# The end of the gates in a hybrid attention block: the last two units' first products, the first heads' operands, the shifts' scores and the gate blocks are placed anew

## Chip, cores, metric

One core of a Trainium2 chip runs the whole block as one program. The metric is the device time of one execution in microseconds; lower is better. Before: 1523.75 us, the median of 3 runs (1515.12 to 1528.22).

## What is computed

One layer of a streaming encoder, 1024 frames of 1024 channels, all in float32. The reference, cut to its skeleton:

```python
h = rms_norm(x, norm1)
qa, ka, va, fa, qc, kc, vc, gates = split(h @ w_in)
o_a = forgetting_attention(qa, ka, va, log_sigmoid(fa + b))   # 8 heads, causal per frame
o_b = chunk_band_attention(qc, kc, vc, rel_bias)              # 8 heads, own and 8 earlier chunks of 64
g_a, g_b = split(sigmoid(gates))
x = x + (g_a * (o_a @ w_branch_a) + g_b * (o_b @ w_branch_b)) @ w_out
x = x + square(relu(rms_norm(x, norm2) @ w_up)) @ w_down
return rms_norm(x, final_norm)
```

What matters here is the boundary between the projection of the gates (2048 channels, 16 blocks of 128) and the attention of the 16 heads.

## The kernel before, in words

**Precision.** Every matrix product is made of two rounded parts of each operand, high and low: hi*hi, hi*lo and lo*hi, so each product of 128 x 128 by 512 is three matmuls (`product`, L211 to L219, the matmul in L218). `split` (L276) makes the parts of an activation, `split_w` (L162) those of a weight: the high part by a copy on ScalarE (L165), the low part by a subtraction (L167), on GpSimd here.

**Units.** The projections run in units of a Strassen-like scheme with seven products (`strassen_steps`, L521). A unit makes two blocks of 128 channels, each in two halves of 512 frames. Its products use the activation operands B11, T2, T1, T3, B21, B22, T4 in this order (`PRODS`) and four PSUM banks; a product is 4 chunks times 3 matmuls, 12 in all. Behind product 0 ScalarE copies the bank (p1), behind products 1 to 3 VectorE adds (L554, L556, L558), behind product 3 a block of output is done, behind product 4 another, behind 5 and 6 an addition (cc, L566) and a block each. `strassen_w` (L172) makes the seven weights from four loaded quarters, with additions on GpSimd (L188, L190, L205, L208) and splits; with `cut` it makes the first two, and the others later from a second load.

**Gates.** Eight units make the gates; `gate_out` (L388) multiplies a block by the frames' norm, takes the sigmoid on ScalarE (L391) and stores it to DRAM. The multiplication (L390) is on VectorE, but for three of the last unit's four blocks (`GPOOL`), which are on GpSimd. Units 0 to 5 come first. Then unit 7's first two products, then unit 6's, then the rest of 7 (L635 to L647). T2 and B11 have their own stack (`xtop`), which is closed when five of unit 6's products have been traced (`EARLY` 6); into that place go the qk tiles of the first two heads (`apq`, 8 KB a partition each, `load_head` L480, 1 MB through GpSimd's queue).

**Shifts.** Ahead of a head's attention the kernel computes a bound of each query's scores (`shifts`, L485): for each of 8 query blocks one or two score pieces of 128 x (128 to 512) on TensorE (L498), each reduced to its least value with the bias by VectorE out of PSUM (L505); then the 8 columns are transposed (L510), split and stored as a row to DRAM (`m_rows`, L513). For a head of the band kind the pieces are 256, 256, 384, 512 and four times 384 + 256 columns, 12 in all. While the attention of head n runs, the shifts of head n + 2 are made; those of the first two heads (`ahead`) are called two steps at a time between the remaining products of units 6 and 7 (`AHEAD` 2), and their banks come from the second half of PSUM (`psd[1]`).

**Attention.** `load_rest` (L693) loads sk (the low parts and the mask rows), v3 (the values) and, last, the shift row from `m_rows` (L700), all through GpSimd's queue. `attend` (L705) makes scores (L725, L733, L741), exponentials (L745), splits them (L277, L278) and accumulates the values (L748 to L750). `forget_columns` (L443) makes eight small transpositions (L449) of the forget sums, which heads 8 to 15 use; it stands ahead of the first head. sk and v3 of both first heads lie in pools that are opened after the operands of the projections have been released (L658). `branch` and `filler` (L667, L682) are products of the band branch that are spread over later heads; their weights (ab) are split when a filler is traced.

**Who sets the order.** A planner orders each engine's instructions by its own estimate of when they are ready; the order in which the program traces them decides between those that are. An instruction given through `TO` (TensorE), `VO` or `AO` is kept behind everything traced before it on its engine; the others may be moved. On the chip each engine takes its instructions in that fixed order. Tiles in released memory wait for the last user of what lay there (`reuse_waits="tile"`).

Of the kernel before, what the change touches and what calls it, by code (L numbers as in the profile page):

```python
# [11 lines left out]
F32 = mybir.dt.float32  # L12
# [6 lines left out]
P = 128  # L19
# [15 lines left out]
EARLY, AHEAD = 6, 2  # L35
# [8 lines left out]
GPOOL = (7,)  # L44
# [38 lines left out]
def hybrid_block(ctx: ExitStack, tc: tile.TileContext, xT, xN, g1, wall, wf, fb, relb, relt, rows, g2, g3, outT):  # L83
# [304 lines left out]
    def gate_out(ps, c, h, eng=V):  # L388
        t = etile("zt")
        eng.tensor_tensor(t, ps, rstd[:, hs(h)], op=ALU.mult)  # L390
        A.activation(t, t, AF.Sigmoid)  # L391
        store(z_dram[c, :, hs(h)], t)
# [92 lines left out]
    def shifts(pr, hh, qk, bc, ps_s, ps_t):  # L485
# [3 lines left out]
        for i in range(8):  # L489
# [17 lines left out]
            if i < 7:  # L507
                yield
        pt = ps_t.tile([P, HALF], F32, tag="d", name="mt")
# [11 lines left out]
    def strassen_steps(u, ps_pool, mk, out, start=(), between=None, before=None, cut=0):  # L521
# [9 lines left out]
        for b in (0, 2, 3, 1) if between else range(4):  # L531
            banks[b] = ps_pool.tile([P, HALF], F32, tag="d", name=f"u{u}_{b}")
# [5 lines left out]
        for i, (n, ks) in enumerate(steps):  # L538
            if i >= cut:
                yield  # L540
            if cut and i == cut:
# [3 lines left out]
            product(banks[b], first and 0 in ks, [((wh[:, k, :], wl[:, k, :]), xop[xn, k]) for k in ks],  # L545
                    3 not in ks)
# [21 lines left out]
        if before:  # L568
            before[1]()
            for a in late:  # L570
                out_(*a)

# [39 lines left out]
    def project_gate(g, **kw):  # L612
        return strassen_steps(U_GATE + g, psd[1 - next(units) % 2], etile,
                              lambda row, h, src: gate_out(src, 2 * g + row, h,
                                                          G if g in GPOOL and (row, h) != (0, 0) else V), **kw)

# [18 lines left out]
    last = project_gate(7, cut=2)  # L635
    next(last)
    steps = project_gate(6)
# [20 lines left out]
    ap_, apv, apq2, ap0 = [pool(astack, n, "right") for n in ("ap", "apv", "apq2", "ap0")]  # L658
# [8 lines left out]
    def branch(ps_pool, b, c, h):  # L667

        if h == 0:
            ab_w[b, c] = [split_w(quarter(U_AB + c // 2, ((0, 1), (3, 2))[c % 2][b]), f"ab{c}_{b}")]  # L670
# [15 lines left out]

    v3 = [apv.tile([P, 8, 3, HD], F32R, tag=f"v3{hh}", name=f"v3{hh}") for hh in range(2)]
    for hh in range(2):
        V.memset(v3[hh][:, :, 2, :].bitcast(F32), 1.0)

    sks = [ap_.tile([SK, 2, S], F32R, tag=f"sk{n}", name=f"sk{n}") for n in range(2)]

    def load_rest(pr, hh):  # L693
        sk = sks[hh]
        if pr % 4 == 0:
            load_r(sk[HD:SK - 2], rows[pr // 4, 0:16])
            load_r(sk[SK - 2:SK, 0, :], rows[pr // 4, 16:18, 0, :])
        load_r(sk[0:HD], sk_dram[2 * pr + hh])
        load_r(v3[hh][:, :, 0:2, :].rearrange("p c a d -> p c (a d)"), v_dram[pr, hh])
        load_r(sk[SK - 2:SK, 1, :], m_rows[2 * pr + hh])  # L700
        return sk
# [3 lines left out]
    def attend(pr, hh, sk, qk, nb):  # L705
# [4 lines left out]
        for h in range(2):  # L710
# [5 lines left out]
            for n, (j, b0, b1) in enumerate(chunks):  # L716
# [8 lines left out]
                T.matmul(ps[:, c], qk[:, 0, keys], qk[:, 1, qs], start=True, stop=False)  # L725
# [37 lines left out]
                yield  # L763
# [21 lines left out]
    forget_columns()  # L785
    rest, steps = load_rest(*heads[0]), iter(())
    for n, hd in enumerate(heads):
        sk, more = rest, iter(())
        if n < 15:
            rest = load_rest(*heads[n + 1])  # L790
        if n < 14:
            tiles.append((load_head(*heads[n + 2]), *load_bias(*heads[n + 2])))
            more = shifts(*heads[n + 2], *tiles[-1][:2], pss, psg)
# [371 lines left out]
```

## Time and profile before

| | us |
|---|---|
| median of the runs | 1523.75 |
| the profiled execution, its own time | 1524.15 |
| its span | 1522.4 |
| TensorE busy (matmuls) | 1462.8 |
| VectorE, ScalarE, GpSimd busy | 950.0, 733.9, 869.1 |
| mean granted clock of TensorE | 0.979 |
| first score piece of the shifts starts | 408.05 |
| last gate product's last matmul starts | 427.71 |
| first attention score (L725) starts | 439.34 |
| first exponential (L745) starts | 441.56 |

The rows are from one profiled execution. PE is TensorE, PEld its weight loads, DVE VectorE, ACT ScalarE, POOL GpSimd, SP the sync engine; a name with q behind it is that engine's queue of issues. A row of the timeline gives start, duration, engine, line, operation, tiles (written <- read), shapes and count; a bracket tells how long the engine had been idle and what released it. Matmul rows overlap by their pipeline, so a rate is read from the distance of two starts.

### The profile page before, as it was taken

What the parts mean: (1) busy time and instruction counts of PE and PEld (TensorE: products, weight loads), DVE (VectorE), ACT (ScalarE), POOL (GpSimd) and SP (SyncE); (2) the same over time, 40 slices, a digit from 0 to 9 for tenths busy, and PEclk for the clock granted to TensorE, in tenths of its full rate; (3) what the DMA queues carried; (4) which work ended last, traced back from release to release, by engine and by line L of the source; (5) the groups of instructions that cost most, each with busy time, mean ns of one, the idle gap of its engine ahead of it and who ended that gap; (6) DMA issues with size and microseconds to landing.
All of it is one profiled execution on the core that took longest, in us unless ns stands there. A gap on an engine that the chain in (4) does not pass through costs nothing.

```text
span 1522.4 us, 20991 instructions
## 1 busy us (share of the span) xinstructions
PE 1462.8 (96%) x6774; PEld 1212.7 (80%) x6774; DVE 950.0 (62%) x1528; ACT 733.9 (48%) x1392; POOL 869.1 (57%) x708
## 2 busy tenths in 40 slices
PE   7999999999888999999999999999999899999996
PEld 5777888888778887888787888888888688888885
DVE  7756555643366777765425677666666457999543
ACT  8533333343358777667425444333333344444653
POOL 2478877777742322121096468888887445567462
PEclk9999999999989899999999999999999999999998
DMA  8546668763589678876567324444443856588363
GB/s 271 151 116 184 190 194 231 195 187 119 173 192 187 156 158 188 200 202 154 165 196 226 127 79 170 152 153 151 153 152 135 278 189 202 155 253 222 97 208 110
DMA packets 153039, 267.18 MB, mean 175 GB/s; under 512 B 22552, under 2 KB 40216, under 8 KB 149792
## 3 DMA queue, kind: packets, MB, share of 16 engines
q1 hardware_dynamic: 78544, 141.02, 30.7%
q10 hardware_dynamic: 50448, 84.27, 17.5%
q0 software_dynamic: 23936, 40.54, 12.5%
q8 instruction: 53, 0.87, 0.2%
q14 instruction: 58, 0.48, 0.1%
HBM read 179.42 MB, written 86.34 MB: 175 GB/s over the span
## 4 chain that ended last, share of the span: by engine, by line
PE 73%; DMA 10%; DVE 6%; POOL 5%; issue 4%; ACT 2%; SPq 0%; ACTq 0%; DVEq 0%; POOLq 0%
PE u L218 36%; PE dS L218 11%; PE dA L218 8%; PE o L218 4%; DMA qk<-qk_dram 3%; PE m L218 2%; DMA wr<-wall 2%; DMA rb<-r_dram 2%; PE pv L748 2%; PE s L498 2%; PE pv L749 1%; PE pv L750 1%; PE st L725 1%; PE st L733 1%; PE dA L96 1%
## 5 line engine op out<-in xcount | busy, mean ns | idle before, releaser
L167 POOL TENSOR_TENSOR wl_A<-wr,wh_A 128x512 fp32r<-128x512 f32 x118 | 166.4, 1418 | 82.1 <-ACT wh_A L165 66.5
L167 POOL TENSOR_TENSOR wl_S<-S,wh_S 128x512 fp32r<-128x512 f32 x102 | 141.1, 1388 | 30.6 <-ACT wh_S L165 30.5
L278 DVE TENSOR_TENSOR tl<-p,th 128x512 fp32r<-128x512 f32 (+1 forms) x192 | 108.8, 586 | 31.2 <-ACT th L277 28.7
L165 ACT CAST wh_A<-wr 128x512 fp32r<-128x512 f32 x105 | 65.0, 620 | 102.0 <-DMA a_dram<-at 52.3
L165 ACT CAST wh_S<-S 128x512 fp32r<-128x512 f32 x105 | 63.6, 618 | 86.8 <-POOL S L190 37.5
L167 POOL TENSOR_TENSOR wl_S<-ks,wh_S 128x512 fp32r<-128x512 f32 x48 | 69.8, 1497 | 51.8 <-ACT wh_S L96 50.3
L277 ACT CAST th<-p 128x512 fp32r<-128x512 f32 (+1 forms) x192 | 93.1, 508 | 11.3 <-PE pv L749 6.9
L505 DVE CUSTOM_DVE_ANT_0 s<-s,bc 128x384 f32<-128x384 f32 (+3 forms) x128 | 69.9, 561 | 42.5 <-PE s L498 29.3
L566 DVE TENSOR_TENSOR cc<-u,u 128x512 f32<-128x512 f32 x70 | 48.1, 688 | 62.9 <-PE u L218 62.8
L498 PE MATMUL s<-qk 128*128 128x384 f32 (+2 forms) x192 | 65.1, 370 | 21.0 <-DMA qk<-qk_dram 14.0
L188 POOL TENSOR_TENSOR S<-wr,wr 128x512 f32<-128x512 f32 x35 | 50.0, 1429 | 56.7 <-DMA wr<-wall 43.3
L927 ACT ACTIVATE v<-v 128x512 f32<-128x512 f32 x64 | 40.5, 632 | 67.4 <-DVE v L926 64.6
L167 POOL TENSOR_TENSOR wl_A<-ka,wh_A 128x512 fp32r<-128x512 f32 x32 | 44.8, 1408 | 48.2 <-ACT wh_A L96 46.7
L748 PE MATMUL pv<-th,v 128*128 128x512 f32 (+1 forms) x192 | 66.4, 346 | 1.1 <-ACT on L761 0.9
L750 PE MATMUL pv<-tl,v 128*128 128x512 f32 (+1 forms) x192 | 66.2, 345 | 0.7 <-DVE tl L278 0.7
L725 PE MATMUL st<-qk 128*128 128x512 f32 (+1 forms) x192 | 66.7, 350 | 0.0
L745 ACT ACTIVATE p<-st,ncq 128x512 f32<-128x512 f32 (+1 forms) x96 | 54.9, 597 | 24.0 <-PE st L741 16.6
L733 PE MATMUL st<-sk 82*128 82x512 f32 (+1 forms) x192 | 66.4, 346 | 0.0
L749 PE MATMUL pv<-th,v 128*64 128x512 f32 (+1 forms) x192 | 65.6, 342 | 0.0
L277 ACT CAST qkh<-qk 128x512 fp32r<-128x512 f32 x32 | 19.9, 621 | 89.2 <-DMA qk_dram<-qkl 37.4
L498 PEld LDWEIGHTS s<-qk 128*128 128x128 f32 x192 | 37.2, 203 | 30.9 <-DMA qk<-qk_dram 14.0
L218 PE MATMUL u<-B21h,wh_A 128*128 128x512 f32 x140 | 55.7, 398 | 1.3 <-ACT p L552 1.3
(401 smaller groups left out, 4961.7 us busy)
## 6 DMA issues: line engine op xcount, KB each, us to landing
wr<-wall SPq DMA_DIRECT2D x243, 256.0 KB
qk<-qk_dram POOLq DMA_DIRECT2D x16, 1024.0 KB, 7.0
a_dram<-at ACTq DMA_DIRECT2D x64, 256.0 KB
xT<-a_dram SPq DMA_DIRECT2D x64, 256.0 KB
qk_dram<-qkh ACTq DMA_DIRECT2D x96, 128.0 KB
a_dram<-v ACTq DMA_DIRECT2D x48, 256.0 KB
xB<-a_dram SPq DMA_DIRECT2D x44, 256.0 KB
z_dram<-zt ACTq DMA_DIRECT2D x32, 256.0 KB
```

What stands on the lines that cost most here:

```text
L165: act.copy(wh, src)
L167: eng.tensor_tensor(wl, src, wh.bitcast(F32), op=ALU.subtract)
L218: eng.matmul(bank, w[wi], x[xi], start=(first and t == 0), stop=(t == n - 1 and not part), skip_group_check=part or not first)
L277: A.copy(dst[0], src)
L278: eng.tensor_tensor(dst[1], src, dst[0].bitcast(F32), op=ALU.subtract)
L498: T.matmul(ps[:, :n], qk[:, 1, i * P:(i + 1) * P], qk[:, 0, ks:ks + n], start=True, stop=not diag)
L505: V.tensor_tensor_reduce(ps[:, :v], ps[:, :v], bc[:, b0:b0 + v], 1.0, prev, ALU.add, ALU.min, out)
L725: T.matmul(ps[:, c], qk[:, 0, keys], qk[:, 1, qs], start=True, stop=False)
L733: T.matmul(ps[:, c], sk[:, 0, keys], sk[:, 1, qs], start=False, stop=not extra)
L748: T.matmul(pv[:, c], v3[hh][:, j, 1:3, :], th[:, c], start=first, stop=False)
L749: T.matmul(pv[0:HD, c], v3[hh][:, j, 0, :], th[:, c], start=False, stop=False)
L750: T.matmul(pv[:, c], v3[hh][:, j, 1:3, :], tl[:, c], start=False, stop=last)
```

## The change

It does six things. (1) `EARLY` is 3: xtop is closed once the first two products of both last units have been traced. (2) The two qk places are swapped, and a pool `ap1` in the same freed memory takes sk and v3 of head 0, whose loads are traced there; the shift row has a load of its own (`load_shift`). (3) PSUM is handed over before the last two units: pools of 1, 4 and 3 banks; unit 7 has its banks where the first, third and second pool give them, the shifts' pieces and transposition have the pool of 3. (4) The products of both units and the first two heads' shifts go through `TO`, with a list of how many steps of the shifts follow each product (in all 16 of 18; a query block is now a step each, the transposition the ninth); the last two follow the first attention score. (5) All gate blocks are multiplied on VectorE. (6) The forget sums' transpositions are traced at head 6, and the copy of the first ab weight is queued behind the last sigmoid.

```diff
-EARLY, AHEAD = 6, 2
+EARLY, AHEAD = 3, (0, 0, 0, 2, 2, 2, 2, 3, 3, 2)
-GPOOL = (7,)
...
-    def gate_out(ps, c, h, eng=V):
+    def gate_out(ps, c, h):
         t = etile("zt")
-        eng.tensor_tensor(t, ps, rstd[:, hs(h)], op=ALU.mult)
-        A.activation(t, t, AF.Sigmoid)
+        V.tensor_tensor(t, ps, rstd[:, hs(h)], op=ALU.mult)
+        sigmoid.append(A.activation(t, t, AF.Sigmoid))
...
-    def shifts(pr, hh, qk, bc, ps_s, ps_t):
+    def shifts(pr, hh, qk, bc, banks, T=T):
-                ps = ps_s.tile([P, HALF], F32, tag="d", name="s")
+                ps = banks["s"].tile([P, HALF], F32, tag="d", name="s")
-            if i < 7:
-                yield
-        pt = ps_t.tile([P, HALF], F32, tag="d", name="mt")
+            yield
+        pt = banks["t"].tile([P, HALF], F32, tag="d", name="mt")
...
-            product(banks[b], first and 0 in ks, [((wh[:, k, :], wl[:, k, :]), xop[xn, k]) for k in ks],
-                    3 not in ks)
+            product(bank(b), first and 0 in ks, [((wh[:, k, :], wl[:, k, :]), xop[xn, k]) for k in ks],
+                    3 not in ks, eng)
...
-    last = project_gate(7, cut=2)
+    pstack.close()
+    lstack = ExitStack()
+    psl, psu, psa = [psum(lstack, n, b) for n, b in (("psl", 1), ("psu", 4), ("psa", 3))]
+    last = project_gate(7, [psl, psa, psu, psu], cut=2, eng=TO)
     next(last)
-    steps = project_gate(6)
+    steps = project_gate(6, [psu] * 4, eng=TO)
     for _ in range(EARLY):
         next(steps)
     xtop.close()
-    apq = [pool(astack, f"apq{n}", "right") for n in range(2)]
+    apq = [pool(astack, f"apq{n}", "right") for n in range(2)][::-1]
+    ap1 = pool(astack, "ap1", "right")
...
+    head_tiles(ap1)
     for n in range(2):
         tiles[n] = (load_head(*heads[n]), *tiles[n])
-    ahead = chain(*[shifts(*heads[n], *tiles[n][:2], psd[1], psd[1]) for n in range(2)])
-    for _ in chain(steps, last):
-        for _ in range(AHEAD):
+    rest = load_rest(*heads[0])
+    s_banks = {"s": psa, "t": psa}
+    ahead = chain(*[shifts(*heads[n], *tiles[n][:2], s_banks, TO) for n in range(2)])
+    for n, _ in enumerate(chain(steps, last)):
+        for _ in range(AHEAD[n]):
             next(ahead, None)
-    for _ in ahead:
-        pass
-    pstack.close()
+    load_shift(*heads[0])
+    lstack.close()
     xstack.close()
...
+        if h == 0 and not ab_w:
+            with tc.issue_after(sigmoid[-1].ins):
+                ab_w[b, c] = [split_w(quarter(U_AB + c // 2, ((0, 1), (3, 2))[c % 2][b]), f"ab{c}_{b}")]
...
+    s_banks.update(s=pss, t=psg)
+    head_tiles(ap_)
...
-    forget_columns()
-    rest, steps = load_rest(*heads[0]), iter(())
+    steps = iter(())
...
+        if 0 < n < 15:
+            load_shift(*heads[n + 1])
+        if n == 6:
+            forget_columns()
...
-        for k, _ in enumerate(attend(*hd, sk, *tiles[n][:3:2])):
+        for k, score in enumerate(attend(*hd, sk, *tiles[n][:3:2])):
+            if n == 0 and k == 0:
+
+                with tc.issue_after(score):
+                    for _ in ahead:
+                        pass
+                load_shift(*heads[1])
```

`head_tiles` allocates one head's sk and v3 and sets v3's ones; `load_rest` and `load_shift` are the old `load_rest` in two parts; `attend` now yields its score's instruction; `bank` in `strassen_steps` allocates a unit's bank when its first product needs it.

More of the change, by code (lines that the diff above doesn't have):

```diff
@@ L530, in strassen_steps, with bank @@
         banks = {}
-        for b in (0, 2, 3, 1) if between else range(4):
-            banks[b] = ps_pool.tile([P, HALF], F32, tag="d", name=f"u{u}_{b}")
+        def bank(b):
+            if b not in banks:
+                banks[b] = (ps_pool[b] if isinstance(ps_pool, list) else ps_pool).tile(
+                    [P, HALF], F32, tag="d", name=f"u{u}_{b}")
+            return banks[b]
+        for b in (0, 2, 3, 1) if between else () if isinstance(ps_pool, list) else range(4):
+            bank(b)
         p1, u2, c22 = mk("p1"), mk("u2"), mk("c22")
```

50 lines of the change are left out of this document (27 added, 23 removed).

## The prediction, on record before the changed kernel ran

> **What bounds the kernel now.** I read the page's totals first, then the busy time by stretches around the edit, then the chain of waits there, then each engine's rows in order of time. The page (busy time, share of the span, instructions):
>
> ```profile
> span 1522.4 us, 20991 instructions
> PE 1462.8 (96%) x6774; PEld 1212.7 (80%) x6774; DVE 950.0 (62%) x1528; ACT 733.9 (48%) x1392; POOL 869.1 (57%) x708
> ```
>
> TensorE is the bound, so what can be won is its idle time and its slow time. The stretches (length, then busy time of PE, PEld, DVE, ACT, POOL, then granted clock, DMA share, GB/s):
>
> ```profile
> 403.00:408.00 5.00, 0.00 (x0) 0.00 (x0) 0.53 (x1) 3.45 (x6) 4.77 (x4) 0.84 0.88 285
> 408.00:428.00 20.00, 19.95 (x80) 16.32 (x80) 11.49 (x29) 4.38 (x7) 15.20 (x18) 0.87 1.20 208
> 428.00:440.00 12.00, 6.85 (x28) 4.75 (x28) 7.68 (x32) 3.39 (x7) 3.79 (x4) 0.74 0.85 304
> 440.00:444.00 4.00, 4.00 (x18) 3.71 (x17) 0.78 (x2) 3.12 (x7) 0.51 (x1) 0.51 0.31 114
> 444.00:760.00 316.00, 299.73 (x1652) 257.32 (x1651) 216.02 (x594) 223.02 (x482) 64.87 (x93) 0.97 0.72 172
> ```
>
> Between gates and attention PE has two holes: all of 403 to 408, and 5.1 of the 12 us to 440; after each, the clock is low. The attention behind it (444 to 760) is PE-bound, 95% busy, so an earlier start of it should survive to the end. The chain names what opens the holes:
>
> ```profile
> 400.57 7.44 DMA qk<-qk_dram
> ...
> 421.80 12.15 DMA qk<-qk_dram
> 434.00 1.66 PE s L498 x5
> ...
> 438.46 0.95 PE cqt L449 x8
> 439.41 1.26 PE st L725 x3
> ```
>
> TensorE's rows in order of time (start, duration; in brackets the idle time and what ended it):
>
> ```profile
> 391.04 0.39 PE L218 MATMUL u<-T1h,wh_S 128*128 128x512 f32 x1
> ...
> 408.05 0.58 PE L498 MATMUL s<-qk 128*128 128x256 f32 x1 [5.07 <-DMA qk<-qk_dram]
> 408.43 0.63 PE L218 MATMUL u<-T4l,wh_A 128*128 128x512 f32 x1
> 408.86 0.63 PE L218 MATMUL u<-T4h,wl_A 128*128 128x512 f32 x1
> ...
> 418.81 0.39 PE L218 MATMUL u<-B21h,wh_A 128*128 128x512 f32 x1
> ...
> 421.55 0.39 PE L218 MATMUL u<-B22h,wh_S 128*128 128x512 f32 x1
> ...
> 429.40 0.27 PE L510 MATMUL mt<-ident,mn 128*8 128x128 f32 x1 [1.30 <-DVE mn L505]
> ...
> 434.00 2.18 PE L498 MATMUL s<-qk 128*128 128x256 f32 x7 [2.16 <-DMA qk<-qk_dram]
> ```
>
> The planner put a shifts' score (s) into the middle of unit 6's last product, and PE, in order, waited for its keys. A gate product is 12 matmuls: 418.81 to 421.55, **2.74 us** at full clock; behind the hole two starts lie 0.43 apart, 5.2 us a product. T2 and B11 are read for the last time before 391.04, where T1 begins. The second hole has the same cause: the score that waits at 434.00 waits for the load issued at 421.80, that of the third head, which nothing needs yet. Then come the last transposition (mt) and the eight transpositions of the forget sums (cqt), and the first attention score at 439.4.
>
> **The change, part by part.** The sum follows PE from unit 6's T1 to the first exponential.
>
> *Two products first, and qk in swapped places.* Unit 7's first two products already stand before unit 6 in the old kernel, and unit 6's follow, so T2 and B11 fall free at the same 391.04: nothing is won there. What changes is the order after it, which is now pinned: four more products of unit 6 (T1, T3, B21, B22) end at 391.04 + 4 x 2.74 = 402.0, and only there stand the first two scores. The qk loads go through POOL's queue:
>
> ```profile
> 395.59 0.74 POOL L482 DMA_DIRECT2D qk<-qk_dram  x1
> ...
> 400.57 0.58 POOL L482 DMA_DIRECT2D qk<-qk_dram  x1
> ...
> 408.29 1.27 POOL L167 TENSOR_TENSOR wl_A<-wr,wh_A 128x512 fp32r<-128x512 f32 x1
> ...
> 415.61 0.55 POOL L696 DMA_DIRECT2D sk<-rows  x1 [1.76 <-PE u L218]
> ...
> 437.18 0.55 POOL L700 DMA_DIRECT2D sk<-m_rows  x1 [5.64 <-DMA m_rows<-mr]
> ```
> ```profile
> DMA to landing us min/median/max: 6.9/6.9/6.9
> ```
>
> The last row is the landing of the load issued at 395.59: 402.5. The old first score waited for the other one (408.0). With the places swapped I take the first head's load as the early one: a wait of 0.5, so scores from **402.5**. Bounds: 0 if the loads pass POOL's weight work, 6.0 if the order stays.
>
> *First head's sk and v in T2's place.* Four more issues (0.55 each by the rows, about 2.2 us) pass through POOL ahead of unit 7's last weights, and 1.2 MB more through the DMA engines between 395 and 410. The last low part (408.29) would end near 412 and is read by the last product, which starts after 420: hidden; without that cover 1 to 3 us. In return these loads no longer wait for T3's reads (415.61).
>
> *Scores between products.* From 402.5 to the first attention score PE must do unit 6's T4 and five products of unit 7, 6 x 2.74 = 16.4; 22 of the 24 score pieces, 7296 columns at the products' price (2.74 us for 12 x 512 columns) = 3.25; one mt 0.3. Without waits: 402.5 + 20.0 = **422.5**. But the pieces have three banks, order is pinned, and four of the seven insertions (2,2,2,2,3,3,2 steps) hold four pieces. The fourth piece waits until VectorE has freed the first, and VectorE first evacuates the product. Its prices:
>
> ```profile
> 436.57 0.60 DVE L505 CUSTOM_DVE_ANT_0 s<-s,bc 128x384 f32<-128x384 f32 x1
> ...
> 437.49 0.49 DVE L505 CUSTOM_DVE_ANT_0 s<-s,bc,st 128x256 f32<-128x256 f32 x1
> ```
> ```profile
> L566 DVE TENSOR_TENSOR cc<-u,u 128x512 f32<-128x512 f32 x4 | 2.8, 692 | 2.4 <-PE u L218 2.4
> ```
> ```profile
> L390 DVE TENSOR_TENSOR zt<-cc,rstd x12: 679/1122/1477, 302.2 to 413.0; 128x512 f32<-128x512 f32 x12
> L390 DVE TENSOR_TENSOR zt<-u,rstd x7: 691/692/692, 298.8 to 421.8; 128x512 f32<-128x512 f32 x7
> ...
> L390 POOL TENSOR_TENSOR zt<-cc,rstd x2: 1272/1274/1275, 427.4 to 429.0; 128x512 f32<-128x512 f32 x2
> ```
>
> Three pieces (384, 256, 384 columns) keep PE 0.46 us. VectorE needs cc 0.69, the gate block 1.0 (between 0.68 and 1.48; POOL is lighter now), the first piece 0.6 (436.57): 2.3 - 0.46 = 1.8 us of waiting. Unit 7's first insertion has one evacuation only (0.69 + 0.6 - 0.46 = 0.8). So 0.8 + 3 x 1.8 = **6.2 us**, first score at **428.7** against 439.4. Bounds: 0 if scores go ahead of evacuations on VectorE, 12.6 if all seven insertions pay 1.8. A full step of two pieces takes VectorE 0.92 (436.57 to 437.49), so its 16 steps are under 15 us of the 26: it stays a source of waits, not the bound.
>
> *Gate blocks on VectorE.* POOL loses 3 x 1.3, VectorE gains 3 x 1.0; all three stand in the 1.8 above. The Trainium skill's SBUF — State Buffer, Who interferes with whom, speaks against it: a tensor_tensor with both inputs in SBUF locks out, or is locked out by, a POOL instruction that reads SBUF. The rows agree (692 from PSUM, up to 1477 from SBUF); with every block at 1.48 the sum would be 1.4 us longer.
>
> *The head's shift row.* mt of head 0 now runs near 418. ACT's rows of before, from its store to the first exponential, and the landing of the load issued at 437.18:
>
> ```profile
> 431.26 0.35 ACTq L513 DMA_DIRECT2D m_rows<-mr  x1
> 431.65 0.63 ACT L391 ACTIVATE zt<-zt 128x512 f32<-128x512 f32 x1 [0.79 <-POOL wl_ab L167]
> 432.31 0.33 ACTq L392 DMA_DIRECT2D z_dram<-zt  x1
> ...
> 439.43 1.28 ACT L745 ACT_TABLE_LOAD   x1 [0.67 <-DVE mr L278]
> ...
> 441.56 0.60 ACT L745 ACTIVATE p<-st 128x512 f32<-128x512 f32 x1 [0.85 <-PE st L741]
> ```
>
> ```profile
> DMA to landing us min/median/max: 1.9/1.9/1.9
> ```
>
> 431.26 to 437.18 is 5.9; with 1.9 to land and 1 before the store (429.40 to 431.26 was 1.9, behind sigmoids) the row is there at 427, 1.7 ahead of its reader. Each microsecond beyond that costs one. The last gate product ends near 426.3; cc, gate block, sigmoid (0.6), its store's issue (0.3) and the table load (1.28) put the first exponential at **430.3**: 11.3 us earlier than 441.56, slightly more than the score, since the four half-speed microseconds after 440 go too.
>
> *Forget columns.* The 0.95 us is inside this gain; in the 95% busy attention it comes back at full clock, 0.5 lost. Holding the first ab split behind the last sigmoid costs nothing seen here: no filler is due before head 9.
>
> Sum against the profiled execution's own 1524.15 us (span and 1.75 around it; 0.4 above the median 1523.75): 1524.15 - 11.3 + 0.5 = **1513.4 us**, 0.7% less.
>
> **The rivals.** *Operands late.* If the first piece still gets the later load, PE stops from 402.5 to 408.0, and one product runs at half clock: 5.5 + 2.4 lost, **1521.3**. For it: POOL's queue order is the planner's, DMA is 88% busy there and gets 1.2 MB more. Against: the swapped places, pinned order. *No bank waits.* Then ACT's tail decides: product end 422.0, plus 0.7 + 0.7 + 0.6 + 0.3 + 1.28, exponential at 425.6: 16.0 - 0.5, **1508.6**. Against it: the program puts evacuations first. *The clock, the slower side.* What it needs:
>
> ```profile
> 433.00:434.00 1.00, 0.00 (x1) 0.00 (x1) 0.43 (x3) 0.38 (x1) 0.00 (x0) 0.85 1.04 406
> 434.00:435.00 1.00, 1.00 (x4) 1.00 (x5) 0.00 (x0) 0.00 (x0) 0.00 (x0) 0.50 1.07 410
> ```
>
> After a 2.16 us hole in a half-busy stretch the clock fell to 0.50. Waits of 1.8 us in every 5 come near that. If it falls at 406 and stays down, five products cost 2.4 more each (12.1), the pieces 2.9, and the bank waits shrink by 4 x 0.46: the first score 13.1 later at 441.8, exponential at 443.4, 1.9 behind the old one, plus 0.5: **1526.5**. It decides from five such products on; three leave a gain. The Trainium skill's TensorE: Matmul & The Clock Gate, Part 1, wants a whole idle window of about 3.4 us before the clock halves; by it this rival is out and the forecast stands. The trace doesn't agree: 2.16 us sufficed. *The order elsewhere.* What isn't pinned is planned anew; PE's 16.3 idle microseconds in 444 to 760 could grow or shrink by half, 8 either way, and more in rare cases.
>
> **How the numbers follow.** Forecast (1509 to 1518) 0.55; late operands 0.20; no bank waits 0.12; clock 0.06; order elsewhere 0.07. The range takes in no bank waits and the late operands and stops between the old time and the clock case: 1505 to 1525. About 1% (15.2 us) is what a measurement tells from no change. Faster by more needs both no bank waits and luck elsewhere, 0.14; slower by more, over 1539, only the rare reordering, 0.05; within, 0.81.
>
> **What would show it.** First attention score near 429, first exponential near 430; scores in blocks between products, none inside one; no PE wait for qk over 1 us; four waits of 0.8 to 1.8 us in the scores, ended by VectorE; clock 1.00 from 391 to 444; no POOL gate block. Wrong would be: a DMA wait over 3 us there, a clock under 0.9 for over 5 us, or an attention that takes more than 5 us longer from its first exponential on.

## The result, and the profile after

The changed kernel takes 1543.38 us (median of 6 runs, 1537.94 to 1549.43) against 1524.67 for the kernel before (6 runs, 1515.12 to 1528.22): a ratio of 1.013, 95% interval 1.0103 to 1.0156. It is slower by 19 us, where 10 us less were forecast, and above the stated range (1505 to 1525). The profiled execution took 1543.94 us. Its page begins:

```profile
span 1542.2 us, 20992 instructions
PE 1463.9 (95%) x6774; PEld 1209.1 (78%) x6774; DVE 961.2 (62%) x1531; ACT 732.3 (47%) x1392; POOL 864.9 (56%) x705
```

TensorE is busy for 1463.9 us, before 1462.8: the work is the same. Its idle time, span less busy time, went from 59.6 to 78.3 us, and these 18.7 us are nearly the whole difference of the spans (19.8). Where they lie is read from busy times by stretches, cut at the first and the last exponential (length, then busy time of PE, PEld, DVE, ACT, POOL, then granted clock, DMA share, GB/s). Before, and after:

```profile
0.00:441.60 441.60, 419.01 (x1850) 340.64 (x1851) 243.83 (x378) 184.58 (x350) 305.97 (x246) 0.98 0.67 187
441.60:735.50 293.90, 278.92 (x1559) 240.76 (x1559) 208.05 (x582) 218.63 (x476) 63.60 (x93) 0.96 0.71 168
```
```profile
0.00:438.50 438.50, 415.43 (x1841) 336.53 (x1841) 251.07 (x375) 183.12 (x346) 297.34 (x240) 1.00 0.66 184
438.50:758.20 319.70, 287.51 (x1566) 245.17 (x1567) 212.91 (x588) 219.02 (x479) 68.94 (x97) 0.95 0.70 160
```

The first exponential comes 3.1 us earlier, not 11.3. From there to the last one the attention takes 319.7 instead of 293.9, and TensorE's idle time in it grows from 15.0 to 32.2. The other 8.6 of these 25.8 us are longer busy time: seven more matmuls stand in the stretch, and the granted clock is 0.95 instead of 0.96. So there are two questions: what took 8 of the 11 us ahead of the attention, and why the attention lost 26.

**Ahead of the attention.** TensorE's rows at the gates' end:

```profile
403.67 0.50 PE L95 MATMUL s<-qk 128*128 128x256 f32 x2 [0.82 <-DMA qk<-qk_dram]
...
412.70 0.38 PE L95 MATMUL s<-qk 128*128 128x256 f32 x1 [2.45 <-DVE mn L506]
413.34 0.44 PE L95 MATMUL s<-qk 128*128 128x384 f32 x1 [0.27 <-DVE mn L506]
415.55 0.58 PE L95 MATMUL s<-qk 128*128 128x256 f32 x1 [1.76 <-DVE st L506]
415.92 0.63 PE L95 MATMUL u<-T3h,wh_S 128*128 128x512 f32 x1
...
433.49 0.39 PE L95 MATMUL s<-qk 128*128 128x256 f32 x1 [0.85 <-DVE st L506]
433.71 0.39 PE L749 MATMUL st<-qk 128*128 128x512 f32 x1
```

(L95 is the helper through which the order written by hand goes.) The swapped qk place worked: the first piece waited 0.82. Then the pieces wait for VectorE, 2.45, 0.27 and 1.76 in a row, and after this hole the matmuls from 415.92 take 0.63: clock 0.52 from 415.90 to 418.90. What VectorE did meanwhile, and GpSimd:

```profile
404.81 6.71 DVE L391 TENSOR_TENSOR zt<-cc,rstd 128x512 f32<-128x512 f32 x1
411.43 0.68 DVE L573 TENSOR_TENSOR cc<-u,u 128x512 f32<-128x512 f32 x1
412.03 0.55 DVE L506 CUSTOM_DVE_ANT_0 s<-s,bc 128x384 f32<-128x384 f32 x1
```
```profile
404.11 0.56 POOL L483 DMA_DIRECT2D qk<-qk_dram  x1
404.68 1.32 POOL L166 TENSOR_TENSOR wl_S<-S,wh_S 128x512 fp32r<-128x512 f32 x1
405.94 1.30 POOL L207 TENSOR_TENSOR S<-wr,S 128x512 f32<-128x512 f32 x1
407.19 1.29 POOL L166 TENSOR_TENSOR wl_S<-wr,wh_S 128x512 fp32r<-128x512 f32 x1
408.45 1.28 POOL L166 TENSOR_TENSOR wl_A<-wr,wh_A 128x512 fp32r<-128x512 f32 x1
409.69 1.26 POOL L166 TENSOR_TENSOR wl_S<-S,wh_S 128x512 fp32r<-128x512 f32 x1
410.92 1.72 POOL L166 TENSOR_TENSOR wl_A<-wr,wh_A 128x512 fp32r<-128x512 f32 x1
```

One gate block, both inputs in SBUF, takes 6.71 us where 0.68 to 1.48 was allowed. It starts (404.81) just behind the first of six GpSimd instructions that stand without a gap, and ends at 411.52; the sixth takes 1.72 instead of 1.3, so by the rows VectorE did its 0.68 around the change from the fifth to the sixth. The scan of the next pieces stood behind it until 412.03. In the kernel before GpSimd had a run without a gap as well, five instructions from 403.23 to 409.56, but the gate block of this product began ahead of it, in a gap of 0.77 us:

```profile
402.84 0.69 DVE L390 TENSOR_TENSOR zt<-cc,rstd 128x512 f32<-128x512 f32 x1
```

Between first score and first exponential lie 4.8 us, before 2.2. ScalarE's rows:

```profile
434.53 0.63 ACT L392 ACTIVATE zt<-zt 128x512 f32<-128x512 f32 x1 [3.15 <-DVE zt L391]
435.07 0.60 ACT L164 CAST wh_ab<-wr 128x512 fp32r<-128x512 f32 x1
435.19 0.33 ACTq L393 DMA_DIRECT2D z_dram<-zt  x1
435.58 1.66 ACT L164 CAST wh_ab<-wr 128x512 fp32r<-128x512 f32 x3
437.25 1.28 ACT L769 ACT_TABLE_LOAD   x1
438.54 0.98 ACT L769 ACTIVATE p<-st 128x512 f32<-128x512 f32 x2
```

The four casts of the ab weight that is held behind the last sigmoid stand ahead of the table load (the load of the exponential's table): 2.2 us.

**In the attention.** The first loss is at once, from head 0 to head 1 (first exponential to first exponential, 11.6 before, 21.8 after):

```profile
443.19 0.39 PE L774 MATMUL pv<-tl,v 128*128 128x512 f32 x1
443.42 0.45 PE L95 MATMUL s<-qk 128*128 128x384 f32 x2
...
445.93 0.27 PE L95 MATMUL mt<-ident,mn 128*8 128x128 f32 x1
...
459.40 0.47 PE L757 MATMUL st<-sk 82*128 82x512 f32 x1 [1.75 <-issue]
```

Head 1's last pieces were to follow the first score. They were traced through the helper that keeps program order, inside the loop over attention steps, so they stand behind everything traced before them, up to the last value matmul of the first step (443.19), which waits for the first exponential. The transposition mt of head 1 comes at 445.93 instead of 438.1; its row is stored at 449.33 and loaded from 452.29 on, landing 7.0 later, 459.3, which is when head 1's first score goes on (459.40; the label "issue" hides this landing). Later rows of the same kind of list, the larger holes only:

```profile
533.90 0.69 PE L499 MATMUL s<-qk 128*128 128x256 f32 x3 [3.79 <-DMA qk<-qk_dram]
...
550.18 0.39 PE L499 MATMUL s<-qk 128*128 128x256 f32 x1 [2.90 <-DMA qk<-qk_dram]
554.79 0.59 PE L450 MATMUL cqt<-ident,cr 8*128 8x8 f32 x4 [0.80 <-DMA cr<-c_dram]
558.87 0.41 PE L450 MATMUL cqt<-ident,cr 8*128 8x8 f32 x4
...
612.05 0.58 PE L499 MATMUL s<-qk 128*128 128x256 f32 x1 [5.92 <-DVE mn L506]
```

Heads 5 and 8 take 32.3 and 27.4 us, before 18.0 and 15.4. In both, two transpositions mt fall into one head, with 27 and 35 matmuls of shift pieces (before: one mt each, with 10 and 21): work for the next heads bunches, and its loads are not there yet. The 5.92 is VectorE standing at the normaliser's load, 5.44 us, with the pieces' scans behind it.

### The profile page after: what moved, and what is told of

It reads as the page before. It is cut to its first block, busy times and chain, and to the rows that moved or that the text cites. A ratio compares the mean times of both kernels' runs of the same rounds, so it can differ in the third digit from the quotient of the medians.

```text
span 1542.2 us, 20992 instructions
## 1 busy us (share of the span) xinstructions
PE 1463.9 (95%) x6774; PEld 1209.1 (78%) x6774; DVE 961.2 (62%) x1531; ACT 732.3 (47%) x1392; POOL 864.9 (56%) x705
## 4 chain that ended last, share of the span: by engine, by line
PE 43%; DMA 2%; DVE 2%; POOL 2%; issue 1%; ACT 1%; SPq 0%; DVEq 0%; ACTq 0%; POOLq 0%
PE u L217 19%; PE dS L217 11%; PE dA L217 8%; PE o L217 4%; PE dA L95 1%; POOL ml L277 1%; DMA m<-m_dram 1%; DMA olt<-o_dram 1%; POOL m L865 1%; DMA rb<-r_dram 0%; DMA wr<-wall 0%; DVE T2l L277 0%; DVE B22l L277 0%; DMA a_dram<-v 0%; PE n_b L248 0%
## 5 line engine op out<-in xcount | busy, mean ns | idle before, releaser
L166 POOL TENSOR_TENSOR wl_S<-S,wh_S 128x512 fp32r<-128x512 f32 x102 | 140.1, 1378 | 32.3 <-ACT wh_S L164 32.1
L276 ACT CAST th<-p 128x512 fp32r<-128x512 f32 (+1 forms) x192 | 93.1, 512 | 14.7 <-PE pv L773 11.0
L499 PE MATMUL s<-qk 128*128 128x512 f32 (+2 forms) x168 | 55.9, 366 | 23.0 <-DMA qk<-qk_dram 12.9
L277 DVE TENSOR_TENSOR qkl<-qk,qkh 128x512 fp32r<-128x512 f32 x32 | 34.7, 1085 | 35.6 <-ACT qkh L276 34.3
L565 DVE TENSOR_TENSOR c<-u,c 128x512 f32<-128x512 f32 x35 | 24.2, 691 | 51.9 <-PE u L217 46.1
```

Source lines behind the costliest of these rows:

```text
L166: eng.tensor_tensor(wl, src, wh.bitcast(F32), op=ALU.subtract)
L276: A.copy(dst[0], src)
L277: eng.tensor_tensor(dst[1], src, dst[0].bitcast(F32), op=ALU.subtract)
L499: T.matmul(ps[:, :n], qk[:, 1, i * P:(i + 1) * P], qk[:, 0, ks:ks + n], start=True, stop=not diag)
```

## The experiments

All times are medians; "of before" is the ratio to the kernel before, run on the same chip, with its 95% interval. The kernel before has medians of 1521 to 1525 in these comparisons, so a difference of 3 us between two kernels says little. Four parts are undone one by one: the pin (the rest of head 1's shifts kept in program order by the helper), the two-input gate sums, the late forget columns and the hold of the ab weight. Every edit is on the changed kernel unless said otherwise.

**First: is the shifts' ninth step the cause?** In the change every shifts has nine steps while a head offers eight calls, so mt falls behind a head's last step. `e1_eight_steps` joins mt to the eighth step in the attention; `e2_nine_steps` gives the kernel before the ninth.

```diff
@@ e1
-            yield
+            if i < 7 or T is TO:
+                yield
@@ e2, in the kernel before
-            if i < 7:
+            if i < 7 or ps_s is not ps_t:
                 yield
```

> The changed kernel, but in the attention a head's last query block and its transposition are one step again (eight steps a head; the first two heads keep nine). Theory 'ninth step': the attention calls eight steps spread over a head and the rest behind it, so the transposition has slipped behind the head's last score, shift rows and the loads queued behind them come late; undone, the attention from the first exponential to the last goes back from 319.7 to near 294 us, and the time from 1543 to 1518 to 1524. Rival 'first heads': the loss is in the first two heads' row and the lock on VectorE; then at most 5 us come back, 1538 to 1543. Rival 'order elsewhere': no cause in this step, any time from 1530 to 1550 with the waits moved about.

> The kernel before, with that one edit alone: in the attention the transposition is a ninth step, the first two heads as they were. Theory 'ninth step': the attention grows by 15 to 25 us, 1540 to 1550. Rivals 'first heads' and 'order elsewhere': within 5 us of before, 1519 to 1529.

e1: 1539.76 (4 runs), 1.0104 (1.0072 to 1.0136). e2: 1522.66 (10 runs), 1.0000 (0.9976 to 1.0023). The ninth step costs the kernel before nothing and gives the change back at most 4 us; the interval of e1's ratio overlaps that of the change (1.0103 to 1.0156). This theory falls.

**The rest of head 1's shifts.** `e3_all_ahead` lets all 18 steps go ahead of the first attention score (last entry of `AHEAD` 4 instead of 2). `f5_free_rest` leaves them where they were traced, without the pin:

```diff
@@ e3
-EARLY, AHEAD = 3, (0, 0, 0, 2, 2, 2, 2, 3, 3, 2)
+EARLY, AHEAD = 3, (0, 0, 0, 2, 2, 2, 2, 3, 3, 4)
@@ f5: shifts, in the loop and ahead of mt
+            T = banks.get("e", T)
...
-    s_banks.update(s=pss, t=psg)
+    s_banks.update(s=pss, t=psg, e=T)
```

> The changed kernel, but all 18 steps of the first two heads' shifts stand ahead of the first attention score (the last entry of the list is 4), instead of two behind it. Theory 'first heads': in the changed kernel head 1 starts 21.8 us behind head 0 instead of 11.6, because its shift row is made at 445.9; made about 10 us earlier, head 1 starts 8 to 10 us earlier for 1 to 2 us of waiting ahead of the first score: 1533 to 1537. Theory 'ninth step' expects the heads behind to keep their loss, so the same 8 to 10; if head 1's late start is paid for by head 0 doing more of the later shifts, nothing comes back: 1541 to 1546.

> The changed kernel, but the two steps of the shifts that are left for the attention are issued through plain TensorE: they must still follow the first attention score, but are no longer kept behind all that was traced before them, the whole first step with its three value products among it. Theory 'the pin': in the changed kernel head 1's last two score pieces stand right behind the first value products (443.19), which wait for the first exponential, and so its row comes late; freed, the pieces follow the score, the transposition comes before 440 instead of 445.9, head 1 starts 12 to 15 us behind head 0 instead of 21.8, and the time is that of all 18 steps ahead (1527.6) or up to 4 us less: 1523 to 1530. Rival 'planner': the planner puts other work ahead of them, 1535 to 1545.

e3: 1527.59 (10 runs), 1.0025 (1.0003 to 1.0047). f5: 1522.04 (10 runs), 0.9997 (0.9973 to 1.0021). e3 gains 16 us where 6 to 10 were expected. Taking the pin away gains 21 us, though f5's first exponential (441.7) is as late as in the kernel before. The pieces now stand where they were meant to, right behind the first scores:

```profile
442.36 0.39 PE L751 MATMUL st<-qk 128*128 128x256 f32 x1 [2.62 <-ACT p L771]
442.88 0.27 PE L512 MATMUL mt<-ident,mn 128*8 128x128 f32 x1
...
445.22 0.74 PE L776 MATMUL pv<-tl,v 128*128 128x512 f32 x1
```

mt of head 1 (442.88) is now ahead of the first pv<-tl (445.22), and head 0 takes 13.4 us instead of 21.8. By the profiled executions its attention is 24.2 us shorter (295.5): 8.4 in head 0, 7.3 in head 5 (25.0 for 32.3) and 8.1 in head 8 (19.3 for 27.4). Its later first exponential costs 3.2 of that.

**The lock.** `e4_in_bank` leaves the sums behind products 3, 5 and 6 of the last two units in PSUM, so that the gate block has one input in SBUF. Product 6 then accumulates onto a changed bank: part of these two units' output blocks isn't the reference's. `f8_free_in_bank` does it behind products 5 and 6 only, whose banks no later product reads, on top of f5:

```diff
+        own = isinstance(ps_pool, list)
...
-                t = mk("cc")
+                t = banks[b] if own else mk("cc")
                 V.tensor_tensor(t, banks[b], u2, op=ALU.add)
```

> The changed kernel, but in the last two units VectorE leaves the sums of products 3, 5 and 6 in their PSUM bank, so the gate block's multiplication has one SBUF input instead of two. Theory 'lock': the multiplication that took 6.71 us while GpSimd ran five instructions back to back takes 0.7, the score pieces behind it wait 1 us instead of 4.3 and the clock stays up: the first score comes 4 to 6 us earlier than 433.7. If the start of the attention carries to the end, 1537 to 1540; if head 1's shift row decides, less than 2 us come back, 1541 to 1545.

> The freed rest of the run before last, and besides the sums of products 5 and 6 of the last two units left in their PSUM banks (product 3's sum goes to SBUF as in the changed kernel). Theories 'pin' and 'lock' together: the 6.7 us multiplication takes 0.7, the first score comes 4 to 6 us earlier, and with head 1's row no longer behind the first value products that gain is kept: 4 to 6 us below the freed rest alone, 1518 to 1525. Rival: the attention takes the gain back (loads and rows aren't earlier), within 2 us of the freed rest alone.

e4: 1533.08 (8 runs), 1.0072 (1.0045 to 1.0100), 10 us less than the change. f8: 1514.54 (10 runs), 0.9955 (0.9929 to 0.9981), 7.5 less than f5. The gate blocks of f8 from 398 us on:

```profile
L391 DVE TENSOR_TENSOR zt<-u,rstd x6: 682/685/692, 399.2 to 426.9; 128x512 f32<-128x512 f32 x6
L391 DVE TENSOR_TENSOR zt<-c,rstd x2: 689/795/901, 397.2 to 414.9; 128x512 f32<-128x512 f32 x2
```
```profile
426.58 0.39 PE L95 MATMUL s<-qk 128*128 128x256 f32 x1 [0.85 <-DVE st L507]
426.80 0.40 PE L752 MATMUL st<-qk 128*128 128x512 f32 x1
```

No block takes over 0.90, and one in the midst of the same six GpSimd instructions, which run from 403.48 to 410.99 here, takes 0.69:

```profile
406.92 0.69 DVE L391 TENSOR_TENSOR zt<-u,rstd 128x512 f32<-128x512 f32 x1
```

The first attention score starts at 426.80 instead of 433.71 (f5, with a lock of 7.51: 436.9). From the first piece to this score f8 needs 24.9 us, 21.1 busy and 3.8 waiting; the change 30.0, of them 23.1 and 6.9. The gain isn't a new order of the work behind it: between the first and the last exponential the matmuls of f5, by tiles and shapes, stand in f8 in the same order, all 1565, and those of the change in e4, all 1566.

**The forget columns and the hold.** `f6_forget_old` puts the transpositions ahead of the first head again; `f7_no_hold` drops the hold.

```diff
@@ f6
+    forget_columns()
     steps = iter(())
...
-        if n == 6:
-            forget_columns()
@@ f7
-        if h == 0 and not ab_w:
-            with tc.issue_after(sigmoid[-1].ins):
-                ab_w[b, c] = [split_w(quarter(U_AB + c // 2, ((0, 1), (3, 2))[c % 2][b]), f"ab{c}_{b}")]
-        elif h == 0:
+        if h == 0:
```

> The changed kernel with the forget sums' transpositions back ahead of the first head. Theory 'forget at head 6': head 5 and 6 together took 45.0 us in the changed kernel against 33.2 before, with a wait for their load among it; put back, 5 to 9 us return for 1 us ahead of the first score: 1535 to 1540. Rival 'nothing': they are hidden or the heads stay late for other reasons: 1541 to 1546.

> The changed kernel without the hold of the first ab weight's copy behind the last sigmoid. Theory 'hold': in the changed kernel four of these copies (435.07 to 437.25) stand between the last sigmoid and the table load, so the first exponential comes 2.2 us late, and with it the row of head 1 behind the first value products; without the hold the first exponential is at 436 to 437 and the time 1539 to 1542. Rival 'no matter': the copies move ahead of the sigmoids and hold up these as much, 1542 to 1546.

f6: 1524.15 (10 runs), 1.0018 (0.9981 to 1.0054): 19 us gained by 1 us of work, at least twice the 5 to 9 expected. f7: 1539.52 (4 runs), 1.0109 (1.0049 to 1.0168): the first exponential comes at 435.2, 3.3 earlier. Of these, 1.8 are there at the first score already (431.9 for 433.7; the longest gate block took 4.91), and 1.5 lie between score and exponential, where the casts stood. By the medians 4 us are gained, but the interval overlaps that of the change. Pin and forget columns together would then be 40 us, more than the change lost. So they can't be two separate prices.

**Do they add?** `g1_rest_forget` undoes both, `g4_rest_forget_bank` the lock as well, `g2_all_undone` the hold too; the edits are those above. `g3_before_forget_late` is the kernel before with one edit:

```diff
-    forget_columns()
...
             rest = load_rest(*heads[n + 1])
+        if n == 6:
+            forget_columns()
```

> The changed kernel with both undone: the rest of head 1's shifts no longer pinned behind the whole first step, and the forget columns ahead of the first head again. Alone they gained 21.3 and 19.2 us of 1543.4. If they are two losses in two places (head 0 to 1, heads 5 to 8), they add: 1503 us, first exponential to last near 283 us. If both only redraw the same order behind them (the late forget columns hurt only where the pin has delayed something), they don't add: 1518 to 1524 us, no better than either alone. Heads 5 and 8 tell where: under 18 and 16 us each by the first, one still over 24 by the second.

> As the one without pin, late forget columns and SBUF sums, but with the hold of the first ab split as the change has it. Separate costs: 1495 us; pin and forget overlapping: 1508 to 1515. Against the same without the hold it gives the hold's price: 4 us longer if the casts stand in front of the table load, 0 if they don't.

> The changed kernel without its four suspected costs: pin, late forget columns, the first ab split's hold behind the last sigmoid, and the sums of products 5 and 6 of the last two units in SBUF (kept in their banks, so the gate block has one SBUF input). If the costs are in separate places: 1522 (pin gone) less 19 (forget) less 7.5 (banks) less up to 4 (hold) = 1492 us, first attention score near 427, first exponential near 430. If pin and forget overlap: 1507 to 1515. If the hold was worth something only because it delayed the order behind it, there is no difference to the same kernel with the hold (within 3 us).

> The kernel before with one part of the change alone: the forget columns made at the seventh head. If their place costs by itself (eight transpositions that wait for a load of about 7 us and hold one of the three score banks): the attention gets 5 to 15 us longer there, and the first attention score comes 0.5 to 1 us earlier: 1528 to 1537. If they hurt only behind the pin: 1520 to 1526, no difference that can be told.

g1: 1526.35 (12 runs), 1.0045 (1.0025 to 1.0066). g4: 1519.89 (12 runs), 0.9995 (0.9967 to 1.0022). g2: 1522.79 (12 runs), 1.0020 (0.9999 to 1.0040). g3: 1534.74 (6 runs), 1.0092 (1.0068 to 1.0115). g1, g2 and g4 lie above every time that was expected for separate or for overlapping costs. They don't add: with the pin gone, the forget columns' old place is 4 us worse than the late one, though in the kernel before the late place costs 13. The lock's price does add (g4 is 6.5 under g1, with the attention's matmuls in the same order), the hold's doesn't (g2 is not under g4).

**A price of the place, or a new order?** The same eight transpositions at other heads, and with their loads early: `h1_forget_5` and `h2_forget_7` change `n == 6` to 5 and 7, `h4_rest_forget_7` to 7 on top of f5; `h3_loads_early` issues the two loads in head 5:

```diff
+    def forget_load():
+        for h in range(2):
+            crs.append(tp.tile([NH, HALF], F32, tag="t", name="cr", bufs=8))
+            load(crs[h], c_dram[:, hs(h)])
...
+            if n == 5 and k == 5:
+                forget_load()
```

> The changed kernel, with the two loads of the forget sums issued half a head earlier (in the sixth head) and only the transpositions left at the seventh. If the late forget columns cost by their loads' landing (about 7 us, while TensorE's order and a score bank wait): 1522 to 1530 us, as with the forget columns at their old place (1524). If they cost by the order that the planner lays around them: anything between 1520 and 1545, and no wait for cr in the trace.

> The changed kernel with the forget columns one head earlier (sixth instead of seventh). Eight transpositions have the same work anywhere. If the place has a price of its own in the late heads: 1540 to 1546 us, as at the seventh. If the cost is a bad draw of the order behind them, the time jumps: more than 5 us off 1543.4, most likely down, 1522 to 1537.

> The changed kernel with the forget columns one head later (eighth instead of seventh). By a price of the late place: 1540 to 1546 us. By a bad draw of the order: more than 5 us off 1543.4, 1522 to 1537.

> The changed kernel with the rest of head 1's shifts free (1522.0 with the forget columns at the seventh head, 1526.4 with them ahead of the first), and the forget columns at the eighth head. A price of the late place gives 1522 again (within 3 us); the order's draw gives anything from 1516 to 1535.

h3: 1543.44 (4 runs), 1.0127 (1.0077 to 1.0177): the loads' landing isn't the price. h1: 1526.06 (10 runs), 1.0012 (0.9988 to 1.0036). h2: 1536.47 (6 runs), 1.0083 (1.0053 to 1.0113). h4: 1519.66 (10 runs), 0.9978 (0.9950 to 1.0006). h4 is within 3 us of f5 and decides nothing by itself. One head earlier takes 17 us away, one head later 7. The work is the same; what differs is the order that the planner lays around it.

The traces show this. Take the matmuls between the first and the last exponential by tiles and shapes, without the forget sums' transpositions, and count the longest sequence that two kernels have in common. The change has 1558; h1 keeps 1190 of them in order, h2 1216, h3 1375, f6 1092. Of the 1558 of the kernel before, g3 keeps 1192, and e2, which costs nothing, all. One pattern goes with the place: with the columns at head 6 (the change, g3, f5, f8 and i2) two mt with 22 to 28 matmuls of pieces fall into head 5; with them at another place (before, f6, g1, h1, h2, h4) there is one mt, with 10 to 13. It isn't the whole price: h3 has one mt and 13 in head 5 too and gains nothing; its head 8 keeps two, with 34.

h1's stretch between first and last exponential:

```profile
437.00:734.20 297.20, 280.46 (x1567) 242.37 (x1568) 210.22 (x588) 219.21 (x479) 68.89 (x97) 0.96 0.69 172
```

It has 1567 matmuls where the change has 1566, and 16.7 us idle instead of 32.2. The pin is still in it and head 0 still takes 21.8, but heads 5 and 8 take 20.4 and 15.7. In the table, attention, idle time and head times are from one profiled execution each; those of f6 (1516.1) and h4 (1514.3) were 8 and 5 us faster than the median:

| kernel | rest | forget at | median | attention | idle in it | heads 0, 5, 8 |
|---|---|---|---|---|---|---|
| before | none left | start | 1524.7 | 293.9 | 15.0 | 11.6, 18.0, 15.4 |
| g3 | none left | head 6 | 1534.7 | 302.1 | 20.9 | 11.6, 28.4, 20.0 |
| changed | pinned | head 6 | 1543.4 | 319.7 | 32.2 | 21.8, 32.3, 27.4 |
| f6 | pinned | start | 1524.2 | 288.9 | 18.4 | 16.5, 17.3, 15.7 |
| h1 | pinned | head 5 | 1526.1 | 297.2 | 16.7 | 21.8, 20.4, 15.7 |
| h2 | pinned | head 7 | 1536.5 | 307.3 | 23.3 | 22.3, 20.0, 15.6 |
| f5 | free | head 6 | 1522.0 | 295.5 | 17.7 | 13.4, 25.0, 19.3 |
| g1 | free | start | 1526.4 | 292.5 | 18.6 | 13.4, 22.1, 10.4 |
| h4 | free | head 7 | 1519.7 | 284.2 | 10.3 | 13.4, 19.8, 14.7 |

**The best of both.** `i1_bank_forget_7` joins h4 and the sums in their banks; `i2_bank_no_hold` takes the hold out of f8.

> The rest of head 1's shifts free, the sums of products 5 and 6 in their banks, and the forget columns at the eighth head. If the two gains are in separate places, the banks take 7 us from 1519.7: 1512 to 1513 us, attention from first to last exponential near 284 us. If the order is drawn anew by the earlier gates, 1512 to 1524, attention over 290 us.

> The rest free, the sums in their banks, the forget columns at the seventh head (1514.5 us), and the first ab split no longer held behind the last sigmoid. If its four casts on ScalarE only delay the first exponential: exponential 1 to 2 us earlier after the last sigmoid and 1511 to 1514 us. If the order is drawn anew, 1510 to 1525.

i1: 1513.49 (8 runs), 0.9939 (0.9914 to 0.9965), faster than both kernels. The lock's removal adds again (6.2 under h4, with the attention's matmuls in the same order). Its page and its attention:

```profile
span 1506.9 us, 20991 instructions
```
```profile
430.80:716.60 285.80, 276.27 (x1558) 237.95 (x1558) 211.74 (x583) 216.38 (x475) 67.64 (x96) 0.97 0.73 179
```

i2: 1525.85 (12 runs), 1.0031 (1.0005 to 1.0057): 11 us more than f8. TensorE and ScalarE at its first scores:

```profile
426.90 0.40 PE L749 MATMUL st<-qk 128*128 128x512 f32 x1
432.92 0.76 PE L757 MATMUL st<-sk 82*128 82x512 f32 x1 [5.63 <-DMA sk<-m_rows]
```
```profile
429.01 1.28 ACT L769 ACT_TABLE_LOAD   x1 [0.67 <-ACT zt L392]
434.15 0.60 ACT L769 ACTIVATE p<-st 128x512 f32<-128x512 f32 x1 [3.86 <-PE st L765]
```

The table is loaded in time, but head 0's shift row lands 5.6 us late: the exponential is at 434.2 instead of 431.6. The freed casts of the ab weight stand ahead of the row's own work on ScalarE:

```profile
419.34 0.62 ACT L164 CAST wh_ab<-wr 128x512 fp32r<-128x512 f32 x1 [0.47 <-DMA wr<-wall]
419.87 0.25 ACT L276 CAST mr<-mt 8x128 fp32r<-8x128 f32 x1
421.84 0.30 ACTq L515 DMA_DIRECT2D m_rows<-mr  x1
```

The transposition mt is at 417.67, in f8 at 417.55; but its copy (mr<-mt) comes at 419.87 instead of 417.86, and so the store at 421.84 instead of 419.62. The row's load is issued 7.8 us behind the store in both (429.60 and 427.43) and lands after 3.2 instead of 1.9 us. The row is the next limit, 2.23 us of waiting in f8 too. The rest of the 11 us lies behind it: 4.7 in the attention (17.0 idle against 12.1) and 3.2 from the last exponential to the end, by the profiled executions.

## Why the prediction was wrong

The sum ran along TensorE to the first exponential and took it as given that "an earlier start of it should survive to the end". **That is the step that failed.** Its reason, 95% busy from 444 to 760, shows that TensorE's work is the bound; it doesn't show that this work comes in the same order. The sign named for it, an attention over 5 us longer, came at 25.8, 17.2 of them idle time of TensorE. Two things were missing in the sum.

- *The rest of head 1's shifts* got no price at all. It was read as following the first score; by the helper's rule it follows all that was traced before, and the next head's shift row, the last thing that head waits for, was 8 us later. Undoing it alone gains 21 us, 8 of them in head 0 by the heads' times.
- *The forget columns* were priced by their work, 0.5 us. In the kernel before, that move alone costs 13, and with the pin kept, putting them back gains 19, moving them one head 17 or 7. The work is as small as it was taken; what costs is the order around it. "The order elsewhere" was a rival, with 8 us either way and a chance of 0.07. It is what happened, at twice the size: 17 us of idle time.

Step by step up to the first exponential:

- *qk in swapped places*: 0.5 forecast, 0.82 found, first piece at 403.67 for 402.5. Right; late operands are out.
- *Scores between products*: 26.2 us forecast from the first piece to the first score, 30.0 in the change. Without the lock it is 24.9 (f8): 21.1 busy for 20.0, waits of 3.8 for 6.2, since a full insertion waits 0.7 to 0.9, not 1.8, once the first one is over (1.37). The size was a little high.
- *"the gate block 1.0 (between 0.68 and 1.48; POOL is lighter now)"*: failed. 6.71 here; 7.57, 6.63, 7.51, 6.84 and 4.91 in e1, e3, f5, f6 and f7. The upper end was the longest row of before, and there no block had waited as long as one GpSimd instruction. In the change two scans of pieces stood ahead of the block, and five DMA issues, four of them new, went through GpSimd's queue from 401.61 to 404.67, where the gap had been. That these brought block and run together is argued from the rows; no run moved them alone. In four pairs of kernels that differ by the two-input sums, 6 to 10 us were gained, with the order of the attention's matmuls unchanged in all four.
- *The Trainium skill's SBUF — State Buffer*, Who interferes with whom, was weighed and given 1.4 us. It says that one engine holds the shared pair for a whole instruction and the other blocks, and that the order of issue decides. The trace agrees that it blocks; it also shows that VectorE need not get the pair when one GpSimd instruction ends and the next is ready: it waited through five (404.68 to 410.95). In f7 a block that began 0.10 us behind the first of the same run took 1.78, so there it got in at the first change. In e1, f5, g1 and h2 the block began 0.7 to 0.8 us ahead of the run, while GpSimd was issuing DMAs, and waited through five all the same. What decides this stays open.
- *The hold "costs nothing seen here"*: the casts stood ahead of the table load, 2.2 us of a path that was forecast as 1.6 and took 4.8. So the hold has a cost, but taking it away isn't a gain: f7 is 4 us faster by medians, not clear of noise, and i2 and g2 gain nothing. In i2 the freed casts delay the shift row.
- *Shift row of head 0*: forecast at 427, loaded at 428.8 with 1.9 to land, 430.7, ahead of its reader at 433.9. In f8 it comes at 429.3 and holds the score for 2.23. The 5.9 from store to load did not hold: 2.2 in the change (426.54 to 428.77), 7.8 in f8 (419.62 to 427.43). Why isn't shown.
- *The clock*: ahead of the first score the half-speed stretch that was feared is there once, for 3 us (0.52), and costs 1.5; f8, whose waits stay at 1.37 or less, has a clock of 1.00 there. But the half-speed microseconds behind the first exponential did not go, as was forecast: from 439.3 to 442.6 the clock is 0.50.

With pin and lock gone (the forget columns late in both), f8 takes 1514.5 and i1 1513.5, where 1513.4 was forecast, with the first exponential at 431.6 and 430.8 for 430.3. So the sum fits the change as it was read, not as it was written. In part that is luck: in f8 the first score comes 1.9 us ahead of the forecast and the exponential follows it after 4.8 us instead of 1.6, and the order behind could have cost more, as g1 and g4 (1526.4, 1519.9) show.

What stays open: which of the planner's estimates turns the order when eight small transpositions move. The runs show that it turns, and in which heads.

## What to carry to other kernels

Where a planner lays the order, a moved step has two prices: its own work, and a new order of all that follows; here the second went to 19 us for 1 us of work, so a few places for the same step are worth a run each, and a sum to the start of a PE-bound stage isn't a sum to its end. When work is put into a loop "behind" an instruction, look at what a pin by program order then makes it wait for, and who reads its result next. A VectorE instruction with two SBUF inputs can be as long as GpSimd's unbroken run beside it: leave one input in PSUM, or look for that run before pricing it by the longest row of the old trace.

## What the runs showed of the hardware

- The wait of a two-input tensor_tensor on VectorE through five GpSimd instructions without a gap: 6.71 us for 0.68 of work, and up to 7.60 (h2). With one input in PSUM a block beside the same run took 0.69 (f8).
- Two holes of 2.45 and 1.76 us with 0.83 us of matmuls among 5.25 were followed by 3 us at a clock of 0.52. The Trainium skill's TensorE: Matmul & The Clock Gate, Part 1, puts the fall behind an idle window of about 3.4 us; here the longest idle time is 2.45 us, and the clock fell all the same.
- The same kernel's executions differ by up to 1.2% (the kernel before, 1512 to 1531 us). f6's profiled execution has a span of 1514.4 while its median is 1524.15, so what a version is worth was taken from medians alone.
